# Products of three parts into one range of 256 PSUM columns, by three matmuls of 256 columns

## The chip, the core and the metric

The kernel runs on one core of one Trainium2 chip, in one launch. The metric is the device time in microseconds (us) of one execution. The engines are named PE (TensorE, the matmuls), PEld (its weight loads), DVE (VectorE), ACT (ScalarE), POOL (GpSimd) and SP (SyncE, which issues the transfers).

## What is computed

Two transformer blocks for 256 tokens and 2048 features, all in float32. Only the skeleton is shown; the mixers hold a gated linear recurrence and a softmax attention (block 1), a gated spatial mixing and a neighbourhood attention (block 2).

```python
def first_block(x, ...):                     # x: (1, 256, 2048)
    h = x + mixer_block(rms_norm(x, norm_mix_w), w_in, ...)   # w_in: 2048 x 11264
    u = rms_norm(h, norm_mlp_w)
    h = h + jnp.square(jax.nn.relu(u @ w_up)) @ w_down        # 2048 x 8192, 8192 x 2048
    return rms_norm(h, norm_final_w)

# inside mixer_block
merged = gate_a * (y_a @ w_branch_a) + gate_b * (y_b @ w_branch_b)
return merged @ w_out

def conv_ffn(x, g_norm, w_up, conv_k, conv_b, w_down):        # second block
    up = rms_norm_2(x, g_norm) @ w_up                         # 2048 x 11008
    up = (pad[:, :t] * conv_k[0] + pad[:, 1:t + 1] * conv_k[1] + pad[:, 2:t + 2] * conv_k[2] + conv_b)
    gate, val = jnp.split(up, 2, axis=-1)
    return x + (jax.nn.silu(gate) * val) @ w_down             # 5504 x 2048
```

## The kernel before

**Exact products from parts.** Every operand of a large product is split into a high and a low part (`split`, lines 100 to 108): ACT copies it into the matmul's format fp32r (line 103, with a scale line 106), which rounds, and DVE subtracts that from the source (line 104, with a scale 107). A product is then the sum of three: high by high, high by low, low by high.

**Feature-major products.** Activations lie with features on the partitions and the 256 tokens along them; of each tile of 128 features the high and the low part lie side by side, 2 x 256 columns (`parts`). `mm3` (lines 121 to 130) multiplies one block of 128 x 128 weights, given as `wh` and `wl`, into one PSUM tile of 512 columns. It issues two matmuls: `wh` with both parts of the activations, 512 columns (line 129), and `wl` with the high part, 256 columns, added to the left half of the PSUM tile (line 130). At the last block of a product the order is turned round (lines 126 and 127). So the left half holds two of the three parts, the right half the third, and whoever reads the tile adds the halves. `unit_b` makes 128 output features from 16 blocks, as two halves of 8 blocks; `unit_branch` and `half_down` use 7 or 8 blocks for one PSUM tile. The PSUM tiles are named `mm`, `mmb` and `mmd`; they come from one pool of four.

**Who reads the tiles.** `joined` (213 to 221): ACT copies the right half (217), DVE adds the left (218), and mostly DVE multiplies by a row of norms or a gate (220). `ev` (the projections, 457 to 466) does the same in its own lines (461, 462, then 464 or 466). `add_to` (223 to 225) adds first the left and then the right half to the residual, both on DVE. In the first feed-forward, `ev_up` takes `joined`, then DVE forms max(z, 0) z (827), then the result is split.

**Token-major products.** `unit_a` (lines 160 to 184) has the three parts as three matmuls of 512 columns each into one PSUM tile `mma` (lines 176 to 178). It makes four of the projections, and isn't touched by the change. The attention and the recurrence have smaller matmuls in full float32, among them line 603.

**The order of the work.** The order is written out by hand: `run` (267 to 309) goes over a list of half units. For each it issues the weight transfer of the half six further on (on SP), splits the weights of the half three further on (`prep`: ACT, then DVE, 128 x 1024), emits the matmuls of this half, and then the evictions that are due (`flush`), mostly of the unit finished one half ago. Background work (attention, recurrence) is emitted a step at a time in between. Every engine runs its own list in that order. PE is busy with the next unit while ACT and DVE read the last.

**The end.** The last product is added to the residual (224, 225), squared (ACT, 314), added up (DVE, 322), summed over the features on PE (333), and the result is scaled and written out.

Of the kernel before, what the change touches and what calls it, by code (L numbers as in the profile page):

```python
# [43 lines left out]
class Builder:  # L44
# [49 lines left out]

# [1 line left out]
    def parts(self, name, n):  # L96
        """n tiles of 128 features by 256 tokens, as a high and a low part side by side."""
        return [self.big_p.tile([P, 4, 2, T], F32R, tag="big", name=self.name(name)) for _ in range(n // 4)]
# [17 lines left out]

# [1 line left out]
    def add(self, x):  # L118
        self.prog.append(x)

    def mm3(self, out, wh, wl, x, start, stop):
        """out[:, :T] + out[:, T:] = w.T @ x"""
        nc = self.nc
        both = x.rearrange("p a t -> p (a t)")
        if stop:
            nc.tensor.matmul(out[:, :T], lhsT=wl, rhs=x[:, 0, :], start=False, stop=False)  # L126
            nc.tensor.matmul(out, lhsT=wh, rhs=both, start=start, stop=True)  # L127
        else:
            nc.tensor.matmul(out, lhsT=wh, rhs=both, start=start, stop=False)  # L129
            nc.tensor.matmul(out[:, :T], lhsT=wl, rhs=x[:, 0, :], start=False, stop=False)  # L130

    def unit_b(self, arr, u, x, evict, delay=1):
        """One tile of 128 output features over 16 tiles of K: out[feature, token]."""
        box = {}

        def emit(i):
            def go(wh, wl):
                if i == 0:
                    box["ps"] = self.mm_p.tile([P, 512], F32, tag="mm", name=self.name("mm"))
                ps = box["ps"]  # L140
                for j in range(8):
                    kt = 8 * i + j
                    w = slice(j * P, (j + 1) * P)
                    self.mm3(ps, wh[:, w], wl[:, w], x(kt), kt == 0, kt == 15)
                if i == 1:
                    self.later(delay, lambda: evict(ps))
            return go

        return [Half(arr[2 * u + i], HALF, emit(i)) for i in range(2)]

    def units(self, units, wave=0):
        """The first halves of the first few go ahead of their second halves."""
        for i in range(2):
            for u in units[:wave]:
                self.add(u[i])
        for u in units[wave:]:
            self.add(u[0])
            self.add(u[1])

    def unit_a(self, arr, u, x, evict, delay=1):  # L160
        """512 output features for both tiles of tokens: out[token, feature]."""
        box = {}
# [37 lines left out]
    def half_down(self, src, n_k, outs, x, evict):  # L200
        """Some output tiles over n_k tiles of K."""
        def go(wh, wl):
            for oi, m in enumerate(outs):
                ps = self.mm_p.tile([P, 512], F32, tag="mm", name=self.name("mmd"))
                for kt in range(n_k):
                    at = (oi * n_k + kt) * P
                    w = slice(at, at + P)
                    self.mm3(ps, wh[:, w], wl[:, w], x(kt), kt == 0, kt == n_k - 1)
                self.later(1, lambda ps=ps, m=m: evict(m, ps))

        self.add(Half(src, n_k * len(outs) * P, go))

    def joined(self, ps, r=None):
        """The two halves of a product, added, and times r."""
        nc = self.nc
        t, z = self.t256("t"), self.t256("z")
        nc.scalar.activation(t, ps[:, T:], AF.Copy)
        nc.vector.tensor_tensor(z, ps[:, :T], t, ALU.add)
        if r is not None:
            nc.vector.tensor_tensor(z, z, r, ALU.mult)  # L220
        return z

    def add_to(self, h, ps):
        self.nc.vector.tensor_tensor(h, ps[:, :T], h, ALU.add)  # L224
        self.nc.vector.tensor_tensor(h, ps[:, T:], h, ALU.add)  # L225

    def later(self, ticks, fn):
        """After some ticks; a generator goes one step each tick."""
        self.due.append((self.tick + ticks, fn))

    def start_bg(self, gen, period=1.0, phases=1):
        """The results that are due after the next half unit are there at the first step.
        With two phases, the second step of a tick comes after the products of the tick."""
        self.bgs.append([gen, period, -1.0, phases, False])
# [75 lines left out]

# [1 line left out]
    def square(self, src, scale=None):  # L312
# [17 lines left out]
    def over_features(self, acc):  # L330
        """The sum over the features for each token, on every partition."""
        ps = self.sm("rs")
        self.nc.tensor.matmul(ps[:, :T], lhsT=self.ones, rhs=acc, start=True, stop=True)
        return ps
# [7 lines left out]
    def newton(self, y, x):  # L342
        """One step towards 1 / sqrt(x)."""
        nc = self.nc
# [5 lines left out]
    def make_r(self, acc, preload=True):  # L350
        """rsqrt(mean over the features + eps) for each token, on every partition."""
        ps = self.over_features(acc)
# [7 lines left out]
    def rows_to_cols(self, r):  # L360
        """A value for each token, as one column for each tile of tokens."""
        nc = self.nc
# [8 lines left out]

# [1 line left out]
    def begin(self, dma, prep):  # L373
# [73 lines left out]

# [1 line left out]
    def x_of(self, key):  # L449
# [3 lines left out]
    def ev(self, key, h, scale=None):  # L453
        nc, st = self.nc, self.st

        def go(ps):
            if h == 0:
                st[key] = self.big(key)
            out = st[key][:, h, :]
            t = self.t256("t")  # L460
            nc.scalar.activation(t, ps[:, T:], AF.Copy)
            nc.vector.tensor_tensor(t, ps[:, :T], t, ALU.add)
            if scale is None:
                nc.vector.tensor_tensor(out, t, st["R"], ALU.mult)
            else:
                nc.vector.scalar_tensor_tensor(out=out, in0=t, scalar=scale, in1=st["R"], op0=ALU.mult, op1=ALU.mult)
        return go
# [13 lines left out]

# [1 line left out]
    def first(self):  # L483
# [192 lines left out]
    def attention(self, n0):  # L676
        """Softmax attention of 16 heads; the first tile of tokens has n0 keys, the second 256."""
        nc, st = self.nc, self.st
# [65 lines left out]

# [1 line left out]
    def merge(self, wga, wgb, w_br, x):  # L746
# [9 lines left out]
        def ev_gate(key, m):  # L756
            def go(ps):
                z = g[key, m] = self.joined(ps, st["R"])
                yield
                nc.scalar.activation(z, z, AF.Sigmoid)  # L760
# [8 lines left out]
        def ev_branch(m):  # L769
            def go(i, ps):  # L770
                g["v", m, i] = self.joined(ps, g.pop(("ga" if i == 0 else "gb", m)))
                if i == 1:
# [13 lines left out]
    def out_proj(self, w_out, resid, gname):  # L786
        """h = residual + merged @ w_out, and its parts for the next product."""
        nc, st = self.nc, self.st
# [27 lines left out]
    def ffn1(self):  # L816
# [4 lines left out]
        def ev_up(c, i):  # L821
            def go(ps):
                if i == 0:
                    acts[c] = self.parts("a", CHUNK)
                z = self.joined(ps, st["R"])
                a = self.t256("a")
                nc.vector.scalar_tensor_tensor(out=a, in0=z, scalar=0.0, in1=z, op0=ALU.max, op1=ALU.mult)
                yield
# [46 lines left out]

# [1 line left out]
    def second(self):  # L877
# [24 lines left out]
        def spill():  # L902
            """The residual of this block: the first block's output."""
            h = st.pop("h")
# [88 lines left out]
    def ffn2(self):  # L993
# [6 lines left out]
        def ev_up(c, i, part):  # L1000
# [3 lines left out]
            def go(ps):  # L1004
                if i == 0 and part == 0:
                    acts[c] = self.parts("a", CHUNK)
                z = self.joined(ps, st["R"])
                yield
# [79 lines left out]

# [1 line left out]
def _b16(w):  # L1090
    """(2048, N) -> halves of units: [2 N/128, 128, 8*128]"""
    k, n = w.shape
# [3 lines left out]
def _a16(w):  # L1096
    """(2048, 1024) -> [2*8, 128, 2*512]"""
    return np.ascontiguousarray(w.reshape(8, 2, P, 2, 512).transpose(3, 0, 2, 1, 4)).reshape(16, P, HALF)
# [10 lines left out]
def _down(w, n):  # L1109
    """(C*n*128, 2048) -> [C*16, 128, n*128]"""  # L1110
    c = w.shape[0] // (n * P)
# [7 lines left out]
def _layout(i):  # L1119
# [33 lines left out]
    a["cvec"] = np.ascontiguousarray(np.concatenate([parts[n] for n in CV], axis=1))  # L1153
    # bias of each pair of a query and a key; keys that a query may not see have a constant
    rb = f("rel_bias")[0]
# [55 lines left out]
```

## Time and profile before

| | |
|---|---|
| median of 2 runs | 2856.62 us (2856.05 to 2857.2) |
| span of the profiled execution | 2855.6 us |
| busy: PE, PEld | 2826.8 us (99%), 2430.9 us (85%) |
| busy: DVE, ACT, POOL | 2032.3 us (71%), 1416.0 us (50%), 117.0 us (4%) |
| matmuls, weight loads | 15876, 15876 |
| granted TensorE clock, mean | 0.997 of full speed (2.4 GHz) |
| moved by DMA | 527.73 MB, mean 185 GB/s |

A busy share says how much of the span an engine had an instruction under way. Matmuls overlap: the next starts while the last still drains, so a matmul's duration in a row is longer than what it costs, and the distance from one start to the next has to be read from the timeline. A weight load is a row of its own (PEld) and overlaps the matmuls.

### The profile page before, as it was taken

To read this page: it belongs to the slowest core of one execution; us is meant where nothing else is said; L and a number is where in the kernel's file an instruction comes from. 1 tells how busy PE (TensorE), PEld (TensorE's weight loads), DVE (VectorE), ACT (ScalarE), POOL (GpSimd) and SP (SyncE) were. 2 spreads that over 40 slices of the span, in tenths; PEclk is the share of its full clock that TensorE was granted. 3 is DMA by queue.
4 is the path that set the end of the run, shared out by engine and by line. 5 is a ranking of instruction groups with operands and counts; after the bars stand their busy time and mean duration, and the time that the engine had idled before them with its cause. 6 is when DMAs were issued, how large, how long until landed. Compare 5 with 4: busy or idle time off the path is not lost.

```text
span 2855.6 us, 41972 instructions
## 1 busy us (share of the span) xinstructions
PE 2826.8 (99%) x15876; PEld 2430.9 (85%) x15876; DVE 2032.3 (71%) x3159; ACT 1416.0 (50%) x2080; POOL 117.0 (4%) x111
## 2 busy tenths in 40 slices
PE   7999999999999999999999999999999999999998
PEld 6888878888888888888888887888888888888886
DVE  6766566766776777667786756676677777777777
ACT  5553555554544444444464445554555544545453
POOL 1031000000100000000030000000010000000000
PEclk9999999999999999999999999999999999999999
DMA  6544554556555555555556665455655555555554
GB/s 215 189 152 148 163 192 154 186 186 219 178 192 186 189 185 185 187 189 185 186 191 214 205 193 184 155 186 186 217 183 190 180 191 185 187 188 180 195 178 140
DMA packets 149387, 527.73 MB, mean 185 GB/s; under 512 B 16704, under 2 KB 19136, under 8 KB 149184
## 3 DMA queue, kind: packets, MB, share of 16 engines
q1 hardware_dynamic: 149184, 525.05, 55.4%
q8 instruction: 125, 2.05, 0.3%
q14 instruction: 78, 0.64, 0.1%
HBM read 520.79 MB, written 4.19 MB: 184 GB/s over the span
## 4 chain that ended last, share of the span: by engine, by line
PE 98%; DVE 1%; ACT 0%; DMA 0%; issue 0%; SPq 0%; DVEq 0%; ACTq 0%
PE mm L129 38%; PE mm L130 19%; PE mmd L129 12%; PE mmd L130 6%; PE mmb L129 4%; PE mm L127 3%; PE mma L176 2%; PE mma L178 2%; PE mma L177 2%; PE mmb L130 2%; PE mmd L127 2%; PE mm L126 1%; PE s L702 1%; PE sc L603 1%; PE mmd L126 1%; PE pt L709 1%
## 5 line engine op out<-in xcount | busy, mean ns | idle before, releaser
L104 DVE TENSOR_TENSOR wl<-raw,wh 128x1024 fp32r<-128x1024 f32 (+2 forms) x973 | 1182.1, 1216 | 752.1 <-ACT wh L103 751.0
L103 ACT ACTIVATE wh<-raw 128x1024 fp32r<-128x1024 f32 (+2 forms) x973 | 1020.9, 1050 | 1328.8 <-issue 481.3
L129 PE MATMUL mm<-u,wh 128*128 128x512 f32 x3090 | 1102.5, 399 | 0.0
L130 PE MATMUL mm<-u,wl 128*128 128x256 f32 x3090 | 867.6, 281 | 0.0
L129 PEld LDWEIGHTS mm<-u,wh 128*128 128x128 f32 x3090 | 580.6, 188 | 136.8 <-issue 3.4
L130 PEld LDWEIGHTS mm<-u,wl 128*128 128x128 f32 x3090 | 583.6, 189 | 9.4
L129 PE MATMUL mmd<-a,wh 128*128 128x512 f32 x1488 | 534.4, 398 | 0.0
L130 PE MATMUL mmd<-a,wl 128*128 128x256 f32 x1488 | 417.6, 281 | 0.0
L129 PE MATMUL mm<-xs,wh 128*128 128x512 f32 x1080 | 392.8, 404 | 7.9 <-DVE xs L107 7.9
L129 PEld LDWEIGHTS mmd<-a,wh 128*128 128x128 f32 x1488 | 279.9, 188 | 57.6
L130 PE MATMUL mm<-xs,wl 128*128 128x256 f32 x1080 | 304.8, 282 | 6.6 <-DVE wl L104 6.6
L130 PEld LDWEIGHTS mmd<-a,wl 128*128 128x128 f32 x1488 | 281.0, 189 | 10.4
L129 PEld LDWEIGHTS mm<-xs,wh 128*128 128x128 f32 x1080 | 204.7, 190 | 55.8 <-DVE xs L107 8.9
L130 PEld LDWEIGHTS mm<-xs,wl 128*128 128x128 f32 x1080 | 205.9, 191 | 10.5 <-DVE wl L104 7.6
L129 PE MATMUL mm<-m,wh 128*128 128x512 f32 x480 | 170.7, 398 | 0.0
L130 PE MATMUL mm<-m,wl 128*128 128x256 f32 x480 | 134.8, 281 | 0.0
L129 PEld LDWEIGHTS mm<-m,wh 128*128 128x128 f32 x480 | 90.2, 188 | 20.7
L225 DVE TENSOR_TENSOR h<-mmd,h 128x256 f32<-128x256 f32 x224 | 95.0, 424 | 7.6
L224 DVE TENSOR_TENSOR h<-mmd,h 128x256 f32<-128x256 f32 x224 | 93.2, 416 | 2.7 <-PE mmd L127 2.7
L130 PEld LDWEIGHTS mm<-m,wl 128*128 128x128 f32 x480 | 90.7, 189 | 1.5
L127 PE MATMUL mmd<-a,wh 128*128 128x512 f32 x224 | 89.3, 399 | 0.0
L127 PE MATMUL mm<-u,wh 128*128 128x512 f32 x206 | 82.3, 399 | 0.0
(239 smaller groups left out, 2939.7 us busy)
## 6 DMA issues: line engine op xcount, KB each, us to landing
raw<-in_w_up SPq DMA_DIRECT2D x300, 512.0 KB, 3.5
raw<-in_w_down SPq DMA_DIRECT2D x128, 512.0 KB, 3.4
raw<-in_w_down SPq DMA_DIRECT2D x80, 448.0 KB, 3.2
raw<-in_w_in_ga SPq DMA_DIRECT2D x64, 512.0 KB, 3.9
raw<-in_w_in_gb SPq DMA_DIRECT2D x64, 512.0 KB, 3.5
raw<-in_w_br SPq DMA_DIRECT2D x64, 512.0 KB, 3.4
raw<-in_w_out SPq DMA_DIRECT2D x64, 512.0 KB, 3.6
raw<-in_w_in_av SPq DMA_DIRECT2D x32, 512.0 KB, 4.2
```

The costliest lines, as they stand in the source:

```text
L103: nc.scalar.activation(hi, src, AF.Copy)
L104: nc.vector.tensor_tensor(lo, src, hi.bitcast(F32), ALU.subtract)
L126: nc.tensor.matmul(out[:, :T], lhsT=wl, rhs=x[:, 0, :], start=False, stop=False)
L127: nc.tensor.matmul(out, lhsT=wh, rhs=both, start=start, stop=True)
L129: nc.tensor.matmul(out, lhsT=wh, rhs=both, start=start, stop=False)
L130: nc.tensor.matmul(out[:, :T], lhsT=wl, rhs=x[:, 0, :], start=False, stop=False)
L176: nc.tensor.matmul(ps, lhsT=xt[:, 0, ts], rhs=wh[:, w], start=kt == 0, stop=False)
L177: nc.tensor.matmul(ps, lhsT=xt[:, 1, ts], rhs=wh[:, w], start=False, stop=False)
L178: nc.tensor.matmul(ps, lhsT=xt[:, 0, ts], rhs=wl[:, w], start=False, stop=kt == 15)
L224: self.nc.vector.tensor_tensor(h, ps[:, :T], h, ALU.add)
L225: self.nc.vector.tensor_tensor(h, ps[:, T:], h, ALU.add)
L603: nc.tensor.matmul(ps[:, hh * P : (hh + 1) * P], lhsT=lhs, rhs=rhs, start=True, stop=True)
```

## The change

`mm3` now issues three matmuls of 256 columns, all into the left half of the PSUM tile: `wl` with the high part first, then `wh` with the low part, then `wh` with the high part, in the same order for each block. The right half isn't used any more, though the tile keeps its 512 columns. So the copy of the right half (ACT) and the addition (DVE) go from `joined`, which becomes `scaled`, and from `ev`; `add_to` has one addition in place of two. In the first feed-forward DVE now forms max(p, 0) r from PSUM in one step (p the product, r the row of norms), and ACT squares it. Comments and docstrings are gone too, by which line numbers move: `mm3`'s matmuls have the lines 125 to 127 in the changed kernel.

```diff
     def mm3(self, out, wh, wl, x, start, stop):
-        """out[:, :T] + out[:, T:] = w.T @ x"""
+
         nc = self.nc
-        both = x.rearrange("p a t -> p (a t)")
-        if stop:
-            nc.tensor.matmul(out[:, :T], lhsT=wl, rhs=x[:, 0, :], start=False, stop=False)
-            nc.tensor.matmul(out, lhsT=wh, rhs=both, start=start, stop=True)
-        else:
-            nc.tensor.matmul(out, lhsT=wh, rhs=both, start=start, stop=False)
-            nc.tensor.matmul(out[:, :T], lhsT=wl, rhs=x[:, 0, :], start=False, stop=False)
+        o = out[:, :T]
+        nc.tensor.matmul(o, lhsT=wl, rhs=x[:, 0, :], start=start, stop=False)
+        nc.tensor.matmul(o, lhsT=wh, rhs=x[:, 1, :], start=False, stop=False)
+        nc.tensor.matmul(o, lhsT=wh, rhs=x[:, 0, :], start=False, stop=stop)
...
-    def joined(self, ps, r=None):
-        """The two halves of a product, added, and times r."""
-        nc = self.nc
-        t, z = self.t256("t"), self.t256("z")
-        nc.scalar.activation(t, ps[:, T:], AF.Copy)
-        nc.vector.tensor_tensor(z, ps[:, :T], t, ALU.add)
-        if r is not None:
-            nc.vector.tensor_tensor(z, z, r, ALU.mult)
+    def scaled(self, ps, r):
+
+        z = self.t256("z")
+        self.nc.vector.tensor_tensor(z, ps[:, :T], r, ALU.mult)
         return z
 
     def add_to(self, h, ps):
         self.nc.vector.tensor_tensor(h, ps[:, :T], h, ALU.add)
-        self.nc.vector.tensor_tensor(h, ps[:, T:], h, ALU.add)
...
             out = st[key][:, h, :]
-            t = self.t256("t")
-            nc.scalar.activation(t, ps[:, T:], AF.Copy)
-            nc.vector.tensor_tensor(t, ps[:, :T], t, ALU.add)
             if scale is None:
-                nc.vector.tensor_tensor(out, t, st["R"], ALU.mult)
+                nc.vector.tensor_tensor(out, ps[:, :T], st["R"], ALU.mult)
             else:
-                nc.vector.scalar_tensor_tensor(out=out, in0=t, scalar=scale, in1=st["R"], op0=ALU.mult, op1=ALU.mult)
+                nc.vector.scalar_tensor_tensor(out=out, in0=ps[:, :T], scalar=scale, in1=st["R"], op0=ALU.mult, op1=ALU.mult)
...
-                z = self.joined(ps, st["R"])
                 a = self.t256("a")
-                nc.vector.scalar_tensor_tensor(out=a, in0=z, scalar=0.0, in1=z, op0=ALU.max, op1=ALU.mult)
+                nc.vector.scalar_tensor_tensor(out=a, in0=ps[:, :T], scalar=0.0, in1=st["R"], op0=ALU.max, op1=ALU.mult)
+                nc.scalar.activation(a, a, AF.Square)
                 yield
                 self.split_x(acts[c], i, a)
```

The other calls of `joined` (gates, branches, the second feed-forward) become calls of `scaled`.

On PE, at the border of two products of the first feed-forward (`mm`: the PSUM tile with its number; `u`: the activations; `wl` and `wh`: the parts of the weights), this stood before:

```order
L129 MATMUL mm_9422<-u_6195,wh_9364 128x512
L130 MATMUL mm_9422<-u_6195,wl_9365 128x256
L126 MATMUL mm_9422<-u_6195,wl_9365 128x256
L127 MATMUL mm_9422<-u_6195,wh_9364 128x512
L129 MATMUL mm_9476<-u_6192,wh_9394 128x512
L130 MATMUL mm_9476<-u_6192,wl_9395 128x256
```

At such a border of the changed kernel's PE list stands now:

```order
L125 MATMUL mm_13220<-u_7294,wl_13149 128x256
L126 MATMUL mm_13220<-u_7294,wh_13148 128x256
L127 MATMUL mm_13220<-u_7294,wh_13148 128x256
L125 MATMUL mm_13286<-u_7291,wl_13185 128x256
L126 MATMUL mm_13286<-u_7291,wh_13184 128x256
L127 MATMUL mm_13286<-u_7291,wh_13184 128x256
```

Six rows of two widths for three blocks of weights have become six rows of one width for two blocks; the second and third of each three have the same weights.

On ACT, in the first feed-forward before (`t`: the copy of the right half; `a_7164`: the split activations, from the tile `a_7171` or `a_7202`; `wh` from `raw`: the weights' split):

```order
L103 ACTIVATE wh_7175<-raw_7084 128x1024
L103 ACTIVATE a_7164<-a_7171 128x256
L217 ACTIVATE t_7197<-mm_7063 128x256
L103 ACTIVATE wh_7206<-raw_7108 128x1024
L103 ACTIVATE a_7164<-a_7202 128x256
```

And on ACT in the changed kernel, at a like place (the square is line 816):

```order
L103 ACTIVATE a_8540<-a_8577 128x256
L816 ACTIVATE a_8613<-a_8613 128x256
L103 ACTIVATE wh_8618<-raw_8500 128x1024
L103 ACTIVATE a_8540<-a_8613 128x256
L103 ACTIVATE wh_8650<-raw_8545 128x1024
```

The square stands where the copy stood, ahead of the next split of weights; it reads a tile that DVE writes, where the copy read PSUM.

## Rows read from the trace of the kernel before

**Rows 1.** The page's head and part 1: busy us (share) xinstructions

```profile
span 2855.6 us, 41972 instructions
PE 2826.8 (99%) x15876; PEld 2430.9 (85%) x15876; DVE 2032.3 (71%) x3159; ACT 1416.0 (50%) x2080; POOL 117.0 (4%) x111
```

**Rows 2.** The page's part 4: the chain that ended last, shares by line

```profile
PE mm L129 38%; PE mm L130 19%; PE mmd L129 12%; PE mmd L130 6%; PE mmb L129 4%; PE mm L127 3%; PE mma L176 2%; PE mma L178 2%; PE mma L177 2%; PE mmb L130 2%; PE mmd L127 2%; PE mm L126 1%; PE s L702 1%; PE sc L603 1%; PE mmd L126 1%; PE pt L709 1%
```

**Rows 3.** PE's waits: who waited for whom: us in total, times, longest us

```profile
PE mm L129 <- DVE xs L107: 7.9, 3, 6.2
PE mm L130 <- DVE wl L104: 6.6, 3, 5.5
```

**Rows 4.** Busy us by stretch (x count): length, PE, PEld, DVE, ACT, POOL, clock, DMA, GB/s

```profile
0.00:60.00 60.00, 45.44 (x228) 37.95 (x229) 41.81 (x53) 32.95 (x48) 13.80 (x15) 0.94 0.64 221
...
800.00:1700.00 900.00, 900.00 (x5021) 779.01 (x5020) 635.40 (x933) 411.01 (x527) 26.02 (x32) 1.00 0.58 191
```

**Rows 5.** The same for lines 129 and 127 alone: PE (x), PEld (x), clock, ...

```profile
0.00:2856.00 2856.00, 2361.10 (x6586) 1239.63 (x6586) 1.00 0.56 185
...
0.00:2856.00 2856.00, 238.44 (x598) 113.25 (x598) 1.00 0.56 185
```

**Rows 6.** Timeline: start us, duration us, engine, line, operation, out<-in, shapes; two products' borders

```profile
999.75 0.28 PE L130 MATMUL mm<-u,wl 128*128 128x256 f32 x1
...
999.87 0.28 PE L126 MATMUL mm<-u,wl 128*128 128x256 f32 x1
...
999.99 0.40 PE L127 MATMUL mm<-u,wh 128*128 128x512 f32 x1
...
1000.23 0.40 PE L129 MATMUL mm<-u,wh 128*128 128x512 f32 x1
1000.23 0.19 PEld L130 LDWEIGHTS mm<-u,wl 128*128 128x128 f32 x1
1000.46 0.28 PE L130 MATMUL mm<-u,wl 128*128 128x256 f32 x1
...
1000.57 0.40 PE L129 MATMUL mm<-u,wh 128*128 128x512 f32 x1
...
1011.18 0.28 PE L126 MATMUL mm<-u,wl 128*128 128x256 f32 x1
```

**Rows 7.** Timeline of PE in a token-major product: the first and the 37th matmul

```profile
344.64 0.39 PE L176 MATMUL mma<-wh,xs 128*128 128x512 f32 x1
...
352.80 0.39 PE L176 MATMUL mma<-wh,xs 128*128 128x512 f32 x1
```

**Rows 8.** Timeline of PE near the start: the first and the 13th L129

```profile
15.03 0.39 PE L129 MATMUL mm<-xs,wh 128*128 128x512 f32 x1
...
19.19 0.39 PE L129 MATMUL mm<-xs,wh 128*128 128x512 f32 x1
```

**Rows 9.** Timeline of PE, 16 matmuls merged; then their group: busy us, mean ns

```profile
233.25 1.95 PE L603 MATMUL sc<-e 128*128 128x128 f32 x16
...
L603 PE MATMUL sc<-e 128*128 128x128 f32 x224 | 27.2, 275 | 0.0
```

**Rows 10.** Groups of DVE and ACT, shapes apart: xcount | busy us, mean ns | idle before

```profile
L225 DVE TENSOR_TENSOR h<-mmd,h 128x256 f32<-128x256 f32 x224 | 95.0, 424 | 7.6
...
L218 DVE TENSOR_TENSOR z<-mm,t 128x256 f32<-128x256 f32 x182 | 75.9, 417 | 0.0
...
L217 ACT ACTIVATE t<-mm 128x256 f32<-128x256 f32 x182 | 66.8, 367 | 0.0
L314 ACT ACTIVATE sq<-h 128x256 f32<-128x256 f32 x64 | 25.8, 404 | 9.2 <-DVE h L225 9.2
```

**Rows 11.** The chain that ended last, in order of time, after the last product

```profile
2841.21 0.02 issue
2841.24 0.43 DVE h L225
```

More of the change, by code (lines that the diff above doesn't have):

```diff
@@ L757, in go @@
             def go(ps):
-                z = g[key, m] = self.joined(ps, st["R"])
+                z = g[key, m] = self.scaled(ps, st["R"])
                 yield
@@ L770, in go @@
             def go(i, ps):
-                g["v", m, i] = self.joined(ps, g.pop(("ga" if i == 0 else "gb", m)))
+                g["v", m, i] = self.scaled(ps, g.pop(("ga" if i == 0 else "gb", m)))
                 if i == 1:
@@ L1006, in go @@
                     acts[c] = self.parts("a", CHUNK)
-                z = self.joined(ps, st["R"])
+                z = self.scaled(ps, st["R"])
                 yield
```

## The prediction

> **What bounds the kernel now.** I read the page first, then the waits of PE, then PE's timeline. PE is busy 99% of the span, and DVE, the next engine, 71% [rows 1]. The chain that ended last runs over PE for 98% of the span, for some 88% on the four lines of `mm3` (126, 127, 129, 130), under the names `mm`, `mmd` and `mmb` [rows 2]. PE's waits for the operands of these products are six, 7.9 + 6.6 us in all [rows 3], and they lie at the start: in the first 60 us PE is busy for 45.44, from 800 to 1700 us for all 900 [rows 4]. So the time is the sum of the distances between starts on PE, and little else: what frees DVE or ACT can bring no more than those 14.5 us.
>
> `mm3` runs 6586 + 598 = 7184 times, at the full granted clock [rows 5]. A matmul's own duration (0.40 or 0.28 us) is no price, since the next starts long before it ends; the distance between starts is. From the L126 at 999.87 to that at 1011.18 lie 32 `mm3` calls: 11.31 / 32 = **353.4 ns for one call** (one product of 512 columns, one of 256) [rows 6]. 7184 x 353.4 ns = 2539 us, 89% of the span. A nanosecond per call is 7.2 us; 2% of the time, about what a measurement here can tell from no change, is 57 us or 8 ns per call. Everything hangs on what three 256-column products cost.
>
> **The change part by part.** *Products.* The same 768 columns per call, in three matmuls instead of two, so three weight loads instead of two: `wh` is loaded twice. Nothing merges these loads in the trace of before: a load stands before each matmul, and starts with the matmul ahead of it (the L130 load at 1000.23, with L129) [rows 6]. A third load therefore must fit into the window of a 256-column product.
>
> How long is a 256-column product c when it follows another? The trace has that at one place, the tile end: L130, L126 and L127 start at 999.75, 999.87 and 999.99, each with weights of its own: **0.12 and 0.12 us** [rows 6]. A second way: the 36 products of 512 columns from 344.64 to 352.80 are 8.16 / 36 = 226.7 ns apart [rows 7], and the fastest long run of L129/L130 calls, 12 of them from 15.03 to 19.19, takes 4.16 / 12 = 346.7 ns a call [rows 8]; 346.7 - 226.7 = 120.0 ns. Both say 120. I take c = 120: a call is 360 ns, 6.6 more than now, and 7184 x 6.6 ns = **+47.4 us**.
>
> No row shows three or more 256-column products of this kind on end, so c is bounded from both sides. Upper: the usual call less a uniform 512-column product, 353.4 - 226.7 = 126.7 ns. Then a call is 380.1, and 7184 x 26.7 ns = +192 us. Lower: half a 512-column product, 113.3 ns (1000.46 to 1000.57 is one such distance, 0.11 [rows 6]): 340 ns, -96 us. Lowest: the L603 run, products of 128 columns in full f32, each with a load: 16 in 1.95 us, the last lasting 0.275, so 1.675 / 15 = 112 ns [rows 9]. That is 336 ns, 7184 x -17.4 ns = -125 us. I stay at 120, because it is the only value at which 256 follows 256 and because the second way meets it.
>
> The Trainium skill ("TensorE: Matmul & The Clock Gate", section "Back-to-back issue gap") prices a matmul in isolation by its columns plus a constant of 2.5 ns, about 109 ns for 256 columns and 216 for 512. By that a call goes from 325 to 327.5 ns, and the sum would be +18 us instead of +47. The trace differs from it: 226.7 ns, not 216, for 512 columns. Its section "LDWEIGHTS (loading the stationary operand)" gives 106.7 ns for 128 columns of weights, nearly the whole window of a 256-column product; no run here shows a load by itself.
>
> *Order inside a call.* `wl` comes first now, at each call. In the steady part weights are split three halves ahead, and PE waits for none. At the start, three of the waits are for `wl` [rows 3], each after a first L129 had gone ahead with `wh`. That one product now waits too: 3 x 0.24 us (1000.23 to 1000.46 is one L129, [rows 6]), **+0.7 us**; nothing at the least, 3 x 0.43 at the most.
>
> *Evictions.* In 342 places (246 calls of `joined`, 96 of `ev`) an ACT copy of 0.367 us and a DVE add of 0.417 go; `add_to` loses one of two adds, 256 x 0.424 us; the first feed-forward also loses a DVE multiply (taken at the 0.424 of that add) in 64 evictions and gets 64 ACT squares of about 0.40 [rows 10]. DVE loses 143 + 109 + 27 = 279 us and ACT 125 - 26 = 99. All of it lies beside PE's products, which wait for none of it, so it costs and gives nothing; were that cover gone, it would be worth its waits, at most 14.5 us. The square stands ahead of the next `wh` split in ACT's queue and waits for the DVE row before it, and behind it are the splits for PE; but those are three halves ahead, some 2.8 us each (eight calls), so a delay of 0.4 us is swallowed.
>
> *End.* The one addition on the chain goes: the L225 at 2841.24 takes 0.43 us and 0.02 of issue [rows 11]: **-0.5 us**.
>
> Sum: 2855.6 + 47.4 + 0.7 - 0.5 = 2903.2 us for the profiled span. The median of the runs, 2856.62, lies 1.0 above the span: **2904 us**.
>
> **The rivals.** *A, the 256-column window is too short.* Place: every product. The trace has a hint. After two 256-column products the 512-column one at 999.99 takes 0.24 us, and the next, at 1000.23, 0.23 [rows 6], against 0.2267 in the uniform run [rows 7]. If that excess is owed by the short windows (the load not ready when the matmul is stamped), then 0.12 is too flattering and the debt is never paid back when no 512-column product follows: c = 126.7, 2855.6 + 192 + 1.2 = 3049 us. It decides from c = 120.4 on, where the time is 2% up; that is a hair above my value. Against it: at 346.7 ns a call no debt is seen, and a uniform stream may settle better than an alternating one, as the 36 products at 226.7 do.
>
> *B, the uniform stream is quicker.* If the alternation itself costs (353.4 against 346.7 in the fast run), uniform 256-column products may fall to 113.3 ns or to the 112 of L603: 2855.6 - 96 + 1.2 = 2761, or 2732. That also covers the case that the second load of the same `wh` costs nothing. Against it: 0.12, twice, with 256 before 256.
>
> *C, the relief of DVE and ACT shows.* At most 14.5 us off the sum, 2890 us. Against it: the waits lie at the start, where no eviction has come yet, and are for `xs` and `wl`. It lies within the forecast's spread.
>
> *D, something is bound that now is not,* such as the supply of PE's instructions, which grow by 45% in rate of matmuls. From c = 128 on, over 3070 us. No row speaks for it.
>
> **How the numbers follow.** Forecast (c from 118 to 122, 2861 to 2947 us): 0.50, of which 0.40 below the 2% line at 120.4 and 0.10 above. A (122 to 127): 0.27. B (112 to 118): 0.17, of which 0.10 below c = 115.1, where it is 2% faster, and 0.07 above. D 0.06; C is inside the forecast. Faster 0.10; same 0.40 + 0.07 = 0.47; slower 0.10 + 0.27 + 0.06 = 0.43. The range goes from 2800 (c = 115.1, leaving 0.10) to 3055 (just above A's 3049, leaving some 0.07). The forecast's own is 2861 to 2947.
>
> **What would show it.** In the profile after, the starts of L125, L126 and L127 should lie 0.12 apart in steady tiles, and 32 calls take 11.5 us; 12.2 says A, 10.9 or less B. PE stays at 99% and the clock full. The `mma` products stay 226.7 ns apart. DVE falls to some 1750 us and ACT to some 1320, without any shift of the end by it. PE's waits for `wl` at the start should grow by under 2 us. The prediction is wrong if a call is not 360 ns, or if PE waits anywhere after the first 60 us.

## The result, and the profile after

| | before | after |
|---|---|---|
| median | 2856.62 us | 2906.99 us (2906.57 to 2907.42, 2 runs) |
| span of the profiled execution | 2855.6 us | 2904.8 us |
| busy: PE, PEld | 2826.8, 2430.9 us | 2878.6, 2819.7 us |
| busy: DVE, ACT | 2032.3, 1416.0 us | 1756.9, 1340.6 us |
| matmuls, weight loads | 15876, 15876 | 23060, 23060 |

The ratio of after to before is 1.0174, with a 95% interval of 1.0157 to 1.0192: the change made the kernel 50 us slower, 1.7%. The forecast was 2904 us.

The page's head and part 1 of the changed kernel (busy us, share, count) answer to [rows 1]:

```profile
span 2904.8 us, 54862 instructions
PE 2878.6 (99%) x23060; PEld 2819.7 (97%) x23060; DVE 1756.9 (60%) x2497; ACT 1340.6 (46%) x1802; POOL 122.7 (4%) x111
```

7184 matmuls more, each with a load of its own: 23060 of both. The weight loads now cover 97% of the span, so hardly a moment is left without one under way. DVE lost 275 us and ACT 75, and PE is busy for 99% of the span, as it was.

Busy us of each engine from 800 to 1700 us, with the clock in the third column from the end; it answers to the second of [rows 4]:

```profile
800.00:1700.00 900.00, 900.00 (x7322) 891.81 (x7322) 515.61 (x662) 399.72 (x502) 29.61 (x32) 1.00 0.61 188
```

PE has no gap and the full clock. So the longer time is a longer distance from start to start. The timeline of PE in the changed kernel, at one place in the first feed-forward (it answers to [rows 6]), with the three products of one call, the first of the next, and the first of the call 32 further on:

```profile
1009.81 0.28 PE L125 MATMUL mm<-u,wl 128*128 128x256 f32 x1
1009.93 0.28 PE L126 MATMUL mm<-u,wh 128*128 128x256 f32 x1
1010.05 0.28 PE L127 MATMUL mm<-u,wh 128*128 128x256 f32 x1
1010.17 0.28 PE L125 MATMUL mm<-u,wl 128*128 128x256 f32 x1
...
1021.33 0.28 PE L125 MATMUL mm<-u,wl 128*128 128x256 f32 x1
```

Each starts 0.12 us after the one ahead of it, and 32 calls take 11.52 us: 360.0 ns a call, where it was 353.4. The token-major products did not move: from the first to the 37th of a run are 8.16 us, 226.7 ns each, as in [rows 7]:

```profile
353.83 0.39 PE L173 MATMUL mma<-wh,xs 128*128 128x512 f32 x1
...
361.99 0.39 PE L173 MATMUL mma<-wh,xs 128*128 128x512 f32 x1
```

### The profile page after: what moved, and what is told of

Its sections match the earlier page's. It is cut to its first block, busy times and chain, and to the rows that moved or that the text cites. A ratio compares the mean times of both kernels' runs of the same rounds, so it can differ in the third digit from the quotient of the medians.

```text
span 2904.8 us, 54862 instructions
## 1 busy us (share of the span) xinstructions
PE 2878.6 (99%) x23060; PEld 2819.7 (97%) x23060; DVE 1756.9 (60%) x2497; ACT 1340.6 (46%) x1802; POOL 122.7 (4%) x111
## 4 chain that ended last, share of the span: by engine, by line
PE 99%; DVE 0%; ACT 0%; DMA 0%; issue 0%; SPq 0%; DVEq 0%; ACTq 0%
PE mm L125 21%; PE mm L126 20%; PE mm L127 20%; PE mmd L127 7%; PE mmd L125 7%; PE mmd L126 7%; PE mmb L127 2%; PE mmb L126 2%; PE mmb L125 2%; PE mma L173 2%; PE mma L174 2%; PE mma L175 2%; PE s L691 1%; PE sc L592 1%; PE pt L698 1%; PE po L705 0%
## 5 line engine op out<-in xcount | busy, mean ns | idle before, releaser
L125 PE MATMUL mm<-u,wl 128*128 128x256 f32 x3296 | 935.2, 284 | 0.0
L126 PE MATMUL mm<-u,wh 128*128 128x256 f32 x3296 | 932.7, 283 | 0.0
L127 PE MATMUL mm<-u,wh 128*128 128x256 f32 x3296 | 932.6, 283 | 0.0
L125 PEld LDWEIGHTS mm<-u,wl 128*128 128x128 f32 x3296 | 632.6, 192 | 3.9 <-issue 3.7
L126 PEld LDWEIGHTS mm<-u,wh 128*128 128x128 f32 x3296 | 632.7, 192 | 0.1
L127 PEld LDWEIGHTS mm<-u,wh 128*128 128x128 f32 x3296 | 632.7, 192 | 0.0
L125 PE MATMUL mmd<-a,wl 128*128 128x256 f32 x1712 | 484.5, 283 | 0.0
L126 PE MATMUL mmd<-a,wh 128*128 128x256 f32 x1712 | 484.5, 283 | 0.0
L127 PE MATMUL mmd<-a,wh 128*128 128x256 f32 x1712 | 484.5, 283 | 0.0
L125 PE MATMUL mm<-xs,wl 128*128 128x256 f32 x1152 | 332.9, 289 | 12.4 <-DVE wl L104 6.5
L127 PEld LDWEIGHTS mmd<-a,wh 128*128 128x128 f32 x1712 | 328.7, 192 | 0.0
L125 PEld LDWEIGHTS mmd<-a,wl 128*128 128x128 f32 x1712 | 328.7, 192 | 0.0
L126 PEld LDWEIGHTS mmd<-a,wh 128*128 128x128 f32 x1712 | 328.7, 192 | 0.0
L126 PE MATMUL mm<-xs,wh 128*128 128x256 f32 x1152 | 328.3, 285 | 0.0
L127 PE MATMUL mm<-xs,wh 128*128 128x256 f32 x1152 | 327.6, 284 | 0.0
L125 PEld LDWEIGHTS mm<-xs,wl 128*128 128x128 f32 x1152 | 222.8, 193 | 15.6 <-DVE wl L104 7.1
L126 PEld LDWEIGHTS mm<-xs,wh 128*128 128x128 f32 x1152 | 222.9, 193 | 0.8 <-DVE xs L107 0.5
L127 PEld LDWEIGHTS mm<-xs,wh 128*128 128x128 f32 x1152 | 222.8, 193 | 0.0
L125 PE MATMUL mm<-m,wl 128*128 128x256 f32 x512 | 144.9, 283 | 0.0
L126 PE MATMUL mm<-m,wh 128*128 128x256 f32 x512 | 144.9, 283 | 0.0
```

What stands on the lines that cost most here:

```text
L125: nc.tensor.matmul(o, lhsT=wl, rhs=x[:, 0, :], start=start, stop=False)
L126: nc.tensor.matmul(o, lhsT=wh, rhs=x[:, 1, :], start=False, stop=False)
L127: nc.tensor.matmul(o, lhsT=wh, rhs=x[:, 0, :], start=False, stop=stop)
```

## The experiments

The theory: a matmul costs its columns plus a constant, so three of 256 columns cost 360 ns, the alternation in the kernel before costs some 7 ns a call that uniform runs don't, and all that DVE and ACT lost lies beside PE. The rivals are named with each run. Two of the questions came up only on the way: whether the 120 ns are a load's time, and what a matmul with a load costs at least.

### The split alone

The kernel before, with the 512-column product as two of 256 in all blocks but the first and the last of each product; ranges, copies and additions as before.

```diff
+        elif start:
+            nc.tensor.matmul(out, lhsT=wh, rhs=both, start=True, stop=False)
+            nc.tensor.matmul(out[:, :T], lhsT=wl, rhs=x[:, 0, :], start=False, stop=False)
         else:
-            nc.tensor.matmul(out, lhsT=wh, rhs=both, start=start, stop=False)
+            nc.tensor.matmul(out[:, :T], lhsT=wh, rhs=x[:, 0, :], start=False, stop=False)
+            nc.tensor.matmul(out[:, T:], lhsT=wh, rhs=x[:, 1, :], start=False, stop=False)
             nc.tensor.matmul(out[:, :T], lhsT=wl, rhs=x[:, 0, :], start=False, stop=False)
```

> The kernel before, with only the matmuls split: in all blocks but the first and the last of each product (5988 of 7184 calls) the product of 512 columns becomes two of 256, into the same two halves of the PSUM tile as before. Copies, additions and evictions stay as they were. Theory (a matmul costs its columns plus a constant, and three of 256 cost 360 ns a call against 353.4): 5988 x 6.6 ns = +40 us, about 2896 us, ratio 1.014. Rival 1 (the loss of the change comes from adding three times in a row into one range of 256 columns): the halves are written apart here, so no loss, 2857 us. Rival 2 (the evictions that the change took away were worth something and hid part of the loss): with the evictions back, the time is above that of the change, over 2907 us.

Measured: 2888.74 us, ratio 1.0111 (1.0096 to 1.0126), span 2886.0. The loss is there without adding three times into one range, and it is some 30 us (30.4 by the spans) instead of 40. That settles rival 1 only if nothing of the change's larger loss is left to it. The timeline of PE in this kernel shows that: the first products of one feed-forward product after the passage from wide (512 columns) to narrow (256), and two places further on in the same run of narrow ones:

```profile
1005.08 0.28 PE L130 MATMUL mm<-u,wl 128*128 128x256 f32 x1
...
1006.25 0.28 PE L132 MATMUL mm<-u,wh 128*128 128x256 f32 x1
...
1010.21 0.28 PE L126 MATMUL mm<-u,wl 128*128 128x256 f32 x1
```

The last 33 steps take 3.96 us, 120.0 ns each, though the halves are written apart: the same price as in the change, so rival 1 falls. The first ten take 1.17 us, 117 ns each: behind wide products narrow ones are quicker for a while, which the sum did not have. For rival 2 the time is below the change's, but this kernel splits fewer calls; what the evictions are worth is settled by the last run below. The last blocks of one product and of the third after it (48 calls, 6 of them unsplit):

```profile
1004.49 0.28 PE L126 MATMUL mm<-u,wl 128*128 128x256 f32 x1
...
1021.67 0.28 PE L126 MATMUL mm<-u,wl 128*128 128x256 f32 x1
```

17.18 us; with the 6 unsplit calls at 353.4 ns, a split one takes 15.06 / 42 = 358.6 ns, some 1.4 less than 360. The products of 8 blocks have only 6 of them split. Two of them on end:

```profile
1050.27 0.28 PE L126 MATMUL mmd<-a,wl 128*128 128x256 f32 x1
...
1055.96 0.28 PE L126 MATMUL mmd<-a,wl 128*128 128x256 f32 x1
```

They take 5.69 us, where two take 2 x 2.82 us in the kernel before (22.56 us for eight, shown further down): 0.05 us over 12 split calls, some 4 ns each and not 6.6. The sum had taken each call as if its neighbours did not matter.

### Wide and narrow products in runs

The kernel before, with the same matmuls in another order inside a product: the 256-column ones stand in one run, between the 512-column ones.

```diff
+    def mm3s(self, out, blocks, start, stop):
...
+        n = len(blocks)
+        cut = n if not stop else 0 if not start else n // 2
+        wide = lambda b, **k: nc.tensor.matmul(out, lhsT=b[0], rhs=b[2].rearrange("p a t -> p (a t)"), **k)
+        for i, b in enumerate(blocks[:cut]):
+            wide(b, start=start and i == 0, stop=False)
+        for b in blocks:
+            nc.tensor.matmul(out[:, :T], lhsT=b[1], rhs=b[2][:, 0, :], start=False, stop=False)
+        for i, b in enumerate(blocks[cut:]):
+            wide(b, start=False, stop=i == n - cut - 1)
```

`blocks` are the high and low weights and the activations of the blocks of one half unit; the three places that called `mm3` block by block call it once.

> The kernel before, same matmuls and evictions, in another order inside a product: the 256-column products with the low part of the weights stand in one run (16 of them in a product of 16 blocks, 8 or 7 in the short ones) between the 512-column ones, instead of alternating with them. Theory (uniform runs cost 226.7 and 120.0 ns a matmul, and the alternation of widths adds the 6.7 ns that a call of 353.4 has above 346.7): each product passes once from narrow to wide, which the trace of before shows to cost 9 + 7 ns there and to give back 7 at the way in; 346.7 + about 1 ns a call, 7184 x -5.9 ns = -42 us, 2814 us, ratio 0.985. Rival (the 353.4 ns belong to the pair of matmuls in whatever order; the tile ends of before, with two narrow and two wide ones in a row, showed no gain): 2857 us, ratio 1.00.

Measured: 2826.71 us, ratio 0.9895 (0.9879 to 0.9912), span 2824.7. It is faster than both kernels: 1.1% below the one before, 80 us below the change. The timeline of PE in it, whole runs merged (start us, duration us, count):

```profile
1000.46 3.82 PE L137 MATMUL mm<-u,wh 128*128 128x512 f32 x16
1004.12 2.08 PE L141 MATMUL mm<-u,wl 128*128 128x256 f32 x16
1006.03 3.82 PE L137 MATMUL mm<-u,wh 128*128 128x512 f32 x16
1009.68 2.08 PE L141 MATMUL mm<-u,wl 128*128 128x256 f32 x16
1011.60 0.63 PE L137 MATMUL mm<-u,wh 128*128 128x512 f32 x2
```

From start to start, two products of 16 blocks take 11.14 us, 348.1 ns a call. A run of 16 wide ones (8 of one product, 8 of the next) takes 3.66 us, 228.8 ns each (uniform: 226.7), a run of 16 narrow ones 1.91, 119.4 each. The order alone changed the time, so the alternation did cost something, and the rival falls. The gain is 30 us where 42 were expected: a product pays some 20 ns for its passages (5.57 us against 16 x 346.7 ns = 5.547), not the 9 put in.

### The second product cut

Three runs of the changed kernel, with fewer columns in the second matmul of each call, so that a part of the product is left out (here 192):

```diff
-        nc.tensor.matmul(o, lhsT=wh, rhs=x[:, 1, :], start=False, stop=False)
+        nc.tensor.matmul(out[:, :192], lhsT=wh, rhs=x[:, 1, :192], start=False, stop=False)
```

> The changed kernel with the second of the three matmuls (high weights by low activations) cut from 256 to 192 columns: this leaves out the low part of 64 tokens. The number of matmuls and of weight loads is the same. Theory (columns plus a constant: from 226.7 ns for 512 and 120.0 for 256 columns, 0.417 ns a column and 13.3 a matmul): that matmul takes 93.3 ns, 7184 x -26.7 ns = -192 us, about 2715 us. Rival (the 120 ns are the time of a weight load, which every matmul needs): no shorter than 112 to 120 ns, 2849 to 2907 us.

> As e3_low_192, with 128 columns: this leaves out the low part of 128 tokens. Theory (columns plus a constant): that matmul takes 66.7 ns, 7184 x -53.3 ns = -383 us, about 2524 us. Rival (a weight load is the floor): the same time as e3_low_192, 2849 to 2907 us. Between the two, if the floor lies between 67 and 93 ns: both runs lie between, and this one gains less over e3_low_192 than 192 us.

> The changed kernel with the second matmul cut to 240 columns: this leaves out the low part of 16 tokens. In e3_low_192 and e4_low_128 the cut matmul's window came to about 109 to 111 ns, whatever its columns. Theory (the price is the larger of columns plus a constant, 113.3 ns for 240 columns, and a load's 109 to 111): at 240 columns the columns still decide, 7184 x -6.7 ns = -48 us against the change, about 2859 us. Rival (120 ns of the uniform stream is itself the load's time, and the 109 to 111 of the cut runs come from another phase): no gain, 2907 us. A third reading (any uneven stream costs some ns a call, as the alternation of before did): 2865 to 2900 us.

Measured: 2828.38 us with 192 columns, 2837.88 with 128, 2813.79 with 240. The theory's 2715 and 2524 are far off. The same view of all three kernels, the first L125 and the 31st, 30 calls on; first with 240 columns:

```profile
1049.89 0.28 PE L125 MATMUL mmd<-a,wl 128*128 128x256 f32 x1
1050.01 0.27 PE L126 MATMUL mmd<-a,wh 128*128 128x240 f32 x1
1050.12 0.28 PE L127 MATMUL mmd<-a,wh 128*128 128x256 f32 x1
...
1060.29 0.28 PE L125 MATMUL mmd<-a,wl 128*128 128x256 f32 x1
```

With 192 columns:

```profile
1049.96 0.28 PE L125 MATMUL mmd<-a,wl 128*128 128x256 f32 x1
1050.08 0.25 PE L126 MATMUL mmd<-a,wh 128*128 128x192 f32 x1
1050.17 0.30 PE L127 MATMUL mmd<-a,wh 128*128 128x256 f32 x1
...
1060.43 0.28 PE L125 MATMUL mmd<-a,wl 128*128 128x256 f32 x1
```

And with 128:

```profile
1049.93 0.28 PE L125 MATMUL mmd<-a,wl 128*128 128x256 f32 x1
1050.05 0.22 PE L126 MATMUL mmd<-a,wh 128*128 128x128 f32 x1
1050.11 0.33 PE L127 MATMUL mmd<-a,wh 128*128 128x256 f32 x1
1050.28 0.28 PE L125 MATMUL mmd<-a,wl 128*128 128x256 f32 x1
...
1060.40 0.28 PE L125 MATMUL mmd<-a,wl 128*128 128x256 f32 x1
```

A call takes 10.40 / 30 = 346.7, 10.47 / 30 = 349.0 and again 349.0 ns. Half of the columns of one matmul are worth 11 ns, not 53. With 128 columns the cut matmul's window shrinks to 0.06 us, and the next one's grows to 0.17: what was cut is waited for one step later. With 128 columns the kernel even took 9.5 us longer than with 192. So there is a floor under each matmul that is not set by its columns. That much was the rival's, though both runs lie below its 2849 to 2907 us; but 16 columns saved 13 ns, which none of the three readings gave for that run: it is under the lowest of them, 2859 us, by 45.

### Two products cut

The changed kernel with the second and the third matmul cut, each to 128 columns (in the diff), or each to the first 240.

```diff
-        nc.tensor.matmul(o, lhsT=wh, rhs=x[:, 1, :], start=False, stop=False)
-        nc.tensor.matmul(o, lhsT=wh, rhs=x[:, 0, :], start=False, stop=stop)
+        nc.tensor.matmul(out[:, :P], lhsT=wh, rhs=x[:, 1, :P], start=False, stop=False)
+        nc.tensor.matmul(out[:, P:T], lhsT=wh, rhs=x[:, 0, P:], start=False, stop=stop)
```

> The changed kernel with the second and the third matmul cut to 128 columns each, one writing the left and one the right quarter of the 512 (half of the high-by-low and half of the high-by-high part are left out). Theory (a weight load sets a floor of 109 to 111 ns for every matmul): a call takes 120 + 2 x 110 = 340 ns, 7184 x -20 ns = -144 us against the change, about 2763 us. Rival (the floor in the cut runs came from one short window between two full ones, and loads can share the time of neighbouring windows): the floor holds for three loads together, 120 + 120 + 110 as in e4_low_128, 2838 us. Without any floor (columns plus a constant): 120 + 2 x 66.7 ns, 2141 us.

> The changed kernel with the second and the third matmul cut to 240 columns: the low part and the high-by-high product of 16 tokens are left out. Theory (one full window and two short ones at the load's floor): 118 to 120 + 2 x 110 ns, 338 to 340 ns a call, 2750 to 2763 us, the same as e6_two_128. Rival (columns plus 13.3 ns): 120 + 2 x 113.3 = 346.7 ns, 2811 us, as e5_low_240.

Measured: 2766.93 us with 128 columns twice, 2784.21 with 240 twice. The timeline of the first of the two, 30 calls:

```profile
1049.82 0.33 PE L125 MATMUL mmd<-a,wl 128*128 128x256 f32 x1
1049.99 0.22 PE L126 MATMUL mmd<-a,wh 128*128 128x128 f32 x1
1050.05 0.28 PE L127 MATMUL mmd<-a,wh 128*128 128x128 f32 x1
1050.16 0.33 PE L125 MATMUL mmd<-a,wl 128*128 128x256 f32 x1
...
1060.02 0.33 PE L125 MATMUL mm<-u,wl 128*128 128x256 f32 x1
```

340.0 ns a call: 256 columns less than the change, and 20 ns less, where the columns alone would be worth 107. That is 120 + 2 x 110, as the theory had it (2763 us), and it is the same floor for each matmul, since a second cut brought another 9 ns. The narrow matmuls in full float32 of the kernel before stood 112 ns apart [rows 9]. So a matmul with a weight load of its own costs about 110 ns here at the least, and the change's 256 columns stand only 10 ns above that. That it is the load which sets the floor is argued and not shown: no run has a matmul without one. With 240 columns twice a call is 10.28 / 30 = 342.7 ns, a little above the 338 to 340 that the theory had, and below the rival's 346.7; the time lies between their 2750 to 2763 and 2811 us, so neither has it right.

### Two more widths

The second matmul alone, with 248 and with 224 columns, as in the first diff of the cut.

> The changed kernel with the second matmul cut to 248 columns: the low part of 8 tokens is left out. e5_low_240 saved 13 ns a call for 16 columns, where the columns account for 6.7. Theory 1 (the columns count double for some reason until the floor): 6.7 ns a call, 7184 x -6.7 ns = -48 us against the change, 2859 us. Theory 2 (only a stream of equal widths settles at 120 ns; once the widths differ, the two full windows fall to about 118 and the short one to 110): a call of 347 to 350 ns again, 2814 to 2835 us. Columns plus a constant: 7184 x -3.3 ns, 2883 us.

> The changed kernel with the second matmul cut to 224 columns: the low part of 32 tokens is left out. Theory (from 240 columns down the load's floor of about 110 ns decides, and the unevenness adds a few ns): between e5_low_240 and e3_low_192, 2814 to 2828 us. Rival (columns go on counting down to here, 6.7 ns below e5_low_240): 2766 us.

Measured: 2842.42 us with 248 columns and 2832.88 with 224; calls of 10.47 / 30 = 349 ns and 10.50 / 30 = 350. Thirty calls are a short stretch. The runs' times say more: what each is below the change's 2906.99 us, divided by 7184 calls (the kernel before, run again beside each group of runs, took 2856.70 to 2857.41 us, so they can be compared). By that a call is 360 ns at 256 columns, 351.0 at 248, 347.0 at 240, 349.7 at 224, 349.1 at 192 and 350.4 at 128: a step at the first cut, and then nothing steady. With 8 columns less than 256 a call is already 9 ns shorter, nearly three times what the columns account for. The run with 248 columns lies between theory 1 (2859 us) and theory 2 (2814 to 2835), nearer to the second; that with 224 is 5 us above its theory's range, and far from the rival's 2766. What makes a wholly uniform stream of 256 columns settle at 120 ns, while one with a narrower matmul in three averages 116 to 117 a matmul, stays open: no run here shows what the load and the stream of columns wait for in each other.

### Order, and the work of the evictions

The changed kernel with the two products of `wh` apart:

```diff
-        nc.tensor.matmul(o, lhsT=wl, rhs=x[:, 0, :], start=start, stop=False)
-        nc.tensor.matmul(o, lhsT=wh, rhs=x[:, 1, :], start=False, stop=False)
-        nc.tensor.matmul(o, lhsT=wh, rhs=x[:, 0, :], start=False, stop=stop)
+        nc.tensor.matmul(o, lhsT=wh, rhs=x[:, 0, :], start=start, stop=False)
+        nc.tensor.matmul(o, lhsT=wl, rhs=x[:, 0, :], start=False, stop=False)
+        nc.tensor.matmul(o, lhsT=wh, rhs=x[:, 1, :], start=False, stop=stop)
```

> The changed kernel with its three matmuls in another order: wh by high, wl by high, wh by low, so that within a call no matmul follows one with the same weights. Theory (each matmul loads its weights anew and pays for it, the same or not): 120 ns each as before, 2907 us, ratio to the kernel before 1.017; the start may move by under 2 us. Rival (the second load of the same weights is partly saved in the changed kernel): slower than 2907 us, by up to some 7184 x 10 ns = 72 us.

Measured: 2906.84 us, ratio 1.0174 (1.0157 to 1.0191), the change's own ratio. Whether the second load of `wh` stands right behind the first or not makes no difference, so the change saved nothing by having them adjacent.

The changed kernel with the copies and additions given back (`ev`, `add_to` and the first feed-forward alike):

```diff
-        z = self.t256("z")
-        self.nc.vector.tensor_tensor(z, ps[:, :T], r, ALU.mult)
+        t, z = self.t256("t"), self.t256("z")
+        self.nc.scalar.activation(t, ps[:, :T], AF.Copy)
+        self.nc.vector.tensor_tensor(z, ps[:, :T], t, ALU.max)
+        self.nc.vector.tensor_tensor(z, z, r, ALU.mult)
```

> The changed kernel with the work given back that the evictions lost: in 342 places an ACT copy out of PSUM and a DVE operation over it and the tile (their maximum, which is the tile itself), a second DVE operation in add_to, and the first feed-forward's old three DVE steps without the square. Theory (all of it lies beside the products): 2907 us, within 3 us, with DVE near 2030 us and ACT near 1415 us busy. Rival (the relief of DVE and ACT bought back part of the products' loss): above 2907 us, by up to the 14 us that PE waited in the kernel before.

Measured: 2908.15 us, ratio 1.0178 (1.0163 to 1.0193). Part 1 of its page:

```profile
PE 2879.9 (99%) x23060; PEld 2820.6 (97%) x23060; DVE 2035.9 (70%) x3159; ACT 1414.7 (49%) x2080; POOL 117.2 (4%) x111
```

DVE and ACT have their 279 and 74 us back, and the time is 1 us above the change's, less than the interval. The work that the change took off them was worth nothing that can be told from noise here.

## Why the prediction was right, point by point

**The bound.** Right: PE at 99%, no gap from 800 to 1700 us, and the whole difference in the distance between starts.

**c = 120 ns.** Right to the nanosecond, 360.0 ns a call over 32 calls, in part by luck. It rested on two readings: two narrow products at the tile ends, and the fastest run of the alternation less a uniform wide product. The first was of the thing itself, but two distances between times rounded to 0.01 us leave 115 to 125 ns each, 15 ns either way in a call of three, or some 108 us either way in the time. The second gave the last digits. It takes the prices of uniform runs to add up in an alternating one, which they do at 346.7 ns a call and do not at the usual 353.4; and a price by columns worked out from the 226.7 and the 120 missed the cut products by over 100 us (2715 against 2828.38). No reason was given why a uniform stream should stay at 120, and the runs leave that open.

**The sum of the products.** 47.4 us was a little low. The 353.4 ns came from products of 16 blocks; those of 8 ran quicker. In the timeline of the kernel before, the last blocks of two `mmd` products, eight products of 8 blocks apart:

```profile
861.56 0.28 PE L126 MATMUL mmd<-a,wl 128*128 128x256 f32 x1
...
884.12 0.28 PE L126 MATMUL mmd<-a,wl 128*128 128x256 f32 x1
```

22.56 / 64 = 352.5 ns a call. All calls became 360, so these lost 7.5 ns and not 6.6. The chains that ended last show what all calls lost together. The last matmul of all these products, before and then after:

```profile
2840.51 0.24 PE mmd L127
...
2890.25 0.13 PE mmd L127
```

It starts 49.74 us later, 0.12 of which come from its place inside its own call (the third matmul now, the second before). The first token-major product, 256 calls on from the start, was 0.70 us later (next point), so the 6927 calls between lost 48.92 us, 7.1 ns each: some 3 us more than 6.6 ns would make. The products of 8 blocks (1664 calls by the counts of their lines) are 1.5 us of that; where the rest lies is open.

**The order inside a call.** Wrong in sign: +0.7 us was put down, and the start gained. The first matmul of the changed kernel, and then its first token-major product:

```profile
5.52 0.58 PE L125 MATMUL mm<-xs,wl 128*128 128x256 f32 x1 [5.52 <-ACT xs L106]
...
111.96 0.40 PE L173 MATMUL mma<-wh,xs 128*128 128x512 f32 x1
```

It started at 5.52 us, where the first 512-column product had waited for the low part of the activations until 6.20: the term counted the wait for `wl`, and forgot that the wide product had to wait for both parts. The first token-major product starts at 111.96 against 111.26, 0.7 later, though 256 calls at 6.6 ns more make 1.7; so the start gave back 1.0. This miss and that of the products went opposite ways, so that the sum came out nearer than its parts. PE's waits for operands there are 12.5 us after, 14.5 before [rows 3]:

```profile
PE mm L125 <- DVE wl L104: 6.5, 3, 5.4
PE mm L125 <- ACT xs L106: 6.0, 2, 5.5
```

**The evictions at nothing.** Right; shown by giving the work back. What ACT would be relieved of was put too high, 99 us where 75 were measured: rows on ACT overlap (before, a split starts at 1000.48 and lasts 1.06 us, and the copy behind it starts at 1001.44), so a copy adds less to the busy time than its 0.37 us. It lies off the path and cost nothing. **The end.** Right: from the addition to the residual to the end of the span, the chain is 14.4 us long after and 14.8 before:

```profile
2890.41 0.44 DVE h L217
2890.92 0.43 ACT sq L306
```

**The rivals.** A, the debt of the short windows, did not come: a uniform stream stays at 120. Its hint was real, but goes with the change of width: the run in groups pays some 20 ns per product there. B's premise was half right: the alternation costs, as the grouped order shows by 30 us; yet uniform narrow products did not fall below 120 in the changed kernel (119.4 in the runs of 16). C and D left no trace: with the work of the evictions back the time is the same, and PE has no gap to wait for instructions in.

## What to carry to other kernels

Where PE has no gap, read what a matmul costs from start to start, and from a place in the trace where that very sequence already occurs, even if it is one tile end in sixteen blocks; count how far the rounding of two starts lets the price range, and get it a second way before the sum hangs on it. Do not carry a price per column from wide products to narrower ones. Splitting a wide product to save work on engines that nobody waits for bought nothing here and paid for one more matmul, with its own load, in each call. If the widths of the products differ, try those of one width in runs before thinking of splitting them: here that was worth 30 us for a change of order alone.

## What was not expected of the hardware

A matmul in fp32r with a load of its own did not start sooner than about 110 ns after the one ahead of it, on average over a call, down to 128 columns: 340.0 ns for 256 + 128 + 128 columns, 349 to 350 for 256 + 128 + 256. And a stream that is uniform at 256 columns was slower by 9 to 13 ns in three matmuls than one in which a single matmul in three is 8 or 16 columns narrower (2842.42 and 2813.79 us against 2906.99). The floor is shown by the runs with 192 and 128 columns and by the two with two matmuls cut; that the load sets it is not, and the cause of the step is open.
